# Row factors out of the gates' small rooms, branch weights behind gates, the last token tile's differences behind two up pairs

## The chip, the cores and the metric

The kernel runs on one core of a Trainium2 chip. The metric is device microseconds of one execution. A core has five engines with instruction queues of their own: TensorE (PE, matmuls; its weight loads are shown as PEld), VectorE (DVE), ScalarE (ACT), GpSimd (POOL) and SyncE (SP), which here only issues DMAs. An instruction waits at the head of its queue for semaphores, and everything behind it on that engine waits with it. Matmul results go to PSUM, which has eight banks of 128 x 512 fp32 here.

## The reference

One encoder layer on 1024 tokens of width 1024, fp32:

```
h = rmsnorm(x, g_mix)
z = h @ w_in                       # pool channels | q | k | v
y_pool = pool_mixer(z[:, :512])    # windows 2, 4, 8, 16: mean - self, per-group linear map, scale
y_attn = diff_attention(q, k, v)   # 8 heads, two softmax maps per head, difference, row-normalized
gates  = sigmoid(h @ w_gate + b_gate)
merged = gates[:, :1024] * (y_pool @ w_branch_pool) + gates[:, 1024:] * (y_attn @ w_branch_attn)
x = x + merged @ w_out
h2 = rmsnorm(x, g_ffn)
x = x + square(relu(h2 @ w_up)) @ w_down
```

## The kernel before

Everything is written in Python against a framework that makes the order of instructions of each engine itself: every instruction carries a priority (`tc.cur_priority`, which grows as the code is written and can be set), a scheduler picks by it and by its own model of when operands are there, and `tc.issue_after(e)` lets what is written inside its block stand only behind instruction `e` in that order. It is no wait for the end of `e`. Buffers are rooms of pools: a tile with a tag gets one of that tag's rooms, and waits until the readers of the room's last holder are done.

fp32 values are multiplied as three products of halves: `split` (L117 to L120) makes the high half by a cast on ACT (L119) and the low half by a subtraction on DVE or POOL (L120), and `mm3` (L125, L126, L127) issues three matmuls into one bank.

The stages, with their place in the profiled execution:

- norm, projections and attention head by head, up to about 700 us. The gates' pre-activations (names g, go) are made as filling work between heads, put into rooms that `tmp` hands out, and stored to DRAM (`g_dram`, L731 and L732). The row factors of a head, 1/norm of its output rows, are transposed (trr), copied (rT, L599) and stored to `r_dram` (L600).
- `y_scaled(d)` (L191 to L198) loads head d's output rows (ry) and its row factors broadcast to all partitions (rb) and multiplies them on DVE. `row_factors(d)` says where the factors lie: in one full room "fu" for d in 0, 1, 2, 3, 5, and in two halves of the small rooms (`tmp`: tags "fr" and "fo", two rooms of 512 columns each for this use) for 4, 6, 7.
- `branch_pool(d)` (L203 to L209), d = 0 to 7, is the pooling branch's product: bp, 192 matmuls from 703.5 to 746.75. Each half of 512 tokens is multiplied in PSUM by its gate on DVE: `mp = bp * gate` (L209). The gate half comes from `gate_half` (L825 to L830): a load from `g_dram` into a small room on SP (L826) and a sigmoid on ACT (L829). `load_cols2` (L145 to L154) brings branch weights for two d at a time (rbp, L148) and splits them on ACT and POOL.
- the attention branch's product, by seven products of sums and differences of quarters (Strassen's scheme): accumulators baX and baY from 747 us, operands wa (from wr, the branch weights) and yb (from ry). Its first accumulators use PSUM banks that bp products have held.
- the output projection (op, about 831 to 923), whose results are added to x in tiles y0 to y7 of 128 tokens, then the second norm. Tiles t = 0 to 3 go through `first_half`, 4 to 7 through `second_half` (L1161): the normalized tile is transposed on PE (hb, L1104) into two banks b12 and b22; `t1 = b12 - r11` and `t2 = b22 - t1` are the operands of two Strassen products; b12 and b22 are copied into the tile's own room (`kept_b`), and `b_split` writes high and low halves. `combine(q)` (L1177) later makes the operands T1, T3, 22 and T4 of tiles 4 to 7 from them; T4 loads d21 back (nd, L1191) into the tile's room.
- 16 up pairs (`up_pair`, a generator that stops twice on its way so that pairs can be interleaved): each is seven products X, Y, Z, W of a pair of column tiles of w_up (wu, L1228) with the quarters of h2, followed by relu, square and stores. X1 and Y (u11) use the quarters of tokens 0 to 511 only; the product with S2 uses T2, Z uses T1, the one with S3 uses T3, W uses 22 and the last T4.
- the down product (Da, Db) to the end.

In the code before, the loop over d writes the weight loads of d + 2 ahead of `branch_pool(d)`; and tiles 4 to 7 are taken one after another through `second_half` with the priorities of their output projections, after which the first steps of pairs 0 to 3 alternate with the four calls of `combine`.

Of the kernel before, what the change touches and what calls it, by code (L numbers as in the profile page):

```python
# [12 lines left out]
ALU = mybir.AluOpType  # L13
# [44 lines left out]
def encoder_kernel(  # L58
# [773 lines left out]
    def row_factors(d):  # L832
        return [fu_tile(f"rb{d}")] if d in (0, 1, 2, 3, 5) else [tmp(f"rb{d}_{i}") for i in range(2)]
# [109 lines left out]
    for d in range(NK):  # L943
        if d % 2 == 0 and d + 2 < NK:
            ws_bp[d + 2] = load_cols2(w_branch_pool, (d + 2) * P, f"bp{d + 2}", fw_tile)
        branch_pool(d, ws_bp[d - d % 2][d % 2], bank)
        if d == 1:
            for k in (6, 7):
                yr[k] = y_scaled(k, row_factors(k))
        if 1 < d < 6:  # L950
            with tc.issue_after(loaded[f"g{d - 1}_1"]):
                load_wr((2, 6, 3, 7)[d - 2])
        if d in (4, 6):
            first_weight_sums(d // 2)
        if d > 4:
            load_a(d - 5)
        if d > 2:
            split_b(d - 3)
# [202 lines left out]
    def second_half(t):  # L1161
        c0 = (t - 4) * P
        t1, t2 = (ev(f"{n}_{t}", (P, 4, P)) for n in ("t1", "t2"))
        T1s[t] = t1
        nc.sync.dma_start(t1, nd[0, t - 4])
        b12, b22 = norm_token(t, lambda j, name: bm.tile([P, 512], F32, tag="ZWY"[j], name=name))
        last["dve"] = dve.tensor_tensor(t1, b12, t1, op=ALU.subtract).ins
        sub(dve, t2, b22, t1)
        kept_b[t] = y[t].rearrange("p (q a b) -> p q a b", q=2, a=4)
        nc.scalar.copy(kept_b[t][:, 0], b12)  # L1170
        nc.scalar.copy(kept_b[t][:, 1], b22)
        b_split("T2", c0, t2, dve)
# [50 lines left out]
    def up_pair(p):  # L1223
# [12 lines left out]
        nc.scalar.copy(x1, X)  # L1236
# [3 lines left out]
        def finish(q, ps, part):  # L1240
            r = ev(f"u{q}_{p}")
            add(dve, r, ps, part)
# [56 lines left out]
    for t in range(4, NT):  # L1299
        tc.cur_priority = prio[min(t + 1, NT - 1)]  # L1300
        second_half(t)
    tc.cur_priority = now
    AHEAD = 4
    for p, q in zip(range(AHEAD), ("T1", "T3", "22", "T4")):
        next(pairs[p])
        if q == "T1":
            next(pairs[0])
        if q == "T3":
            body = tc.cur_priority
        with ExitStack() as behind:  # L1310
# [199 lines left out]
```

## Time and profile before

| | |
|---|---|
| median of 3 runs | 1547.08 us (1545.67 to 1551.84) |
| the profiled execution, its own time | 1546.83 us |
| span of its instructions | 1545.0 us |
| PE busy | 1517.9 us (98%), 7601 matmuls |
| DVE, ACT, POOL busy | 1065.1, 824.6 and 328.2 us |

The span is the time from the first to the last instruction in the profile, 1.83 us shorter than the execution. In the timelines a row is start and duration in us, engine, line, operation, output <- inputs, shape and count, and in brackets how long the engine had been idle and what released it; "SPq" and "ACTq" rows are DMA issues. In the list of waits a row has total, number and longest wait in us. Window rows have the stretch, its length, busy us with instruction counts of PE, PEld, DVE, ACT and POOL, the granted clock, the share of the DMA engines and GB/s. Rows of DMA issues end with KB each and the median us from issue to landing. Matmuls are pipelined: a duration of 0.39 us goes with a distance of 0.225 us from one to the next.

### The profile page before, as it was taken

What the parts mean: (1) busy time and instruction counts of PE and PEld (TensorE: products, weight loads), DVE (VectorE), ACT (ScalarE), POOL (GpSimd) and SP (SyncE); (2) the same over time, 40 slices, a digit from 0 to 9 for tenths busy, and PEclk for the clock granted to TensorE, in tenths of its full rate; (3) what the DMA queues carried; (4) which work ended last, traced back from release to release, by engine and by line L of the source; (5) the groups of instructions that cost most, each with busy time, mean ns of one, the idle gap of its engine ahead of it and who ended that gap; (6) DMA issues with size and microseconds to landing.
All of it is one profiled execution on the core that took longest, in us unless ns stands there. A gap on an engine that the chain in (4) does not pass through costs nothing.

```text
span 1545.0 us, 22233 instructions
## 1 busy us (share of the span) xinstructions
PE 1517.9 (98%) x7601; PEld 1312.5 (85%) x7601; DVE 1065.1 (69%) x2361; ACT 824.6 (53%) x1821; POOL 328.2 (21%) x476
## 2 busy tenths in 40 slices
PE   7999999999999999999899998999999999999998
PEld 6999999899999999788688887888888888888887
DVE  7777777778788887844678648766666668556672
ACT  6666565666565666543464556556555634333331
POOL 6654572434343334221000112000000000000000
PEclk9999999999999999999999999999999999999999
DMA  7331331111212022536455733555343699537750
GB/s 244 119 110 59 100 103 49 58 55 44 66 37 75 20 73 78 203 103 225 143 204 186 252 109 122 177 174 174 133 140 109 238 335 392 192 123 258 225 191 28
DMA packets 172045, 221.12 MB, mean 143 GB/s; under 512 B 10950, under 2 KB 104859, under 8 KB 171931
## 3 DMA queue, kind: packets, MB, share of 16 engines
q1 hardware_dynamic: 154522, 192.39, 37.8%
q10 hardware_dynamic: 17408, 27.30, 4.7%
q8 instruction: 60, 0.98, 0.3%
q14 instruction: 55, 0.44, 0.1%
HBM read 157.76 MB, written 61.90 MB: 142 GB/s over the span
## 4 chain that ended last, share of the span: by engine, by line
PE 90%; DMA 4%; DVE 3%; issue 1%; ACT 1%; SPq 0%; POOL 0%; ACTq 0%; DVEq 0%; POOLq 0%
PE z L127 6%; PE z L125 6%; PE z L126 6%; PE Da L125 4%; PE Da L126 4%; PE Da L127 4%; PE g L125 3%; PE g L126 3%; PE g L127 3%; PE Db L126 3%; PE Db L125 3%; PE Db L127 3%; PE X L125 3%; PE X L127 3%; PE X L126 3%; PE sc L486 2%
## 5 line engine op out<-in xcount | busy, mean ns | idle before, releaser
L127 PE MATMUL z<-wqkv,hT 128*128 128x384 f32 x512 | 174.3, 341 | 0.6 <-DVE hT L120 0.6
L125 PE MATMUL z<-wqkv,hT 128*128 128x384 f32 x512 | 174.6, 342 | 0.1
L126 PE MATMUL z<-wqkv,hT 128*128 128x384 f32 x512 | 174.3, 341 | 0.0
L496 ACT ACTIVATE s<-s,nm 128x256 f32<-128x256 f32 (+7 forms) x128 | 99.7, 779 | 69.9 <-DVE nm L488 61.5
L125 PE MATMUL g<-hT,fwgate 128*128 128x512 f32 x256 | 100.8, 394 | 0.7 <-ACT go L731 0.7
L126 PE MATMUL g<-hT,fwgate 128*128 128x512 f32 x256 | 100.6, 393 | 0.0
L125 PEld LDWEIGHTS z<-wqkv,hT 128*128 128x128 f32 x512 | 96.9, 189 | 3.8 <-ACT hT L119 0.4
L127 PE MATMUL g<-hT,fwgate 128*128 128x512 f32 x256 | 99.9, 392 | 0.0
L127 PEld LDWEIGHTS z<-wqkv,hT 128*128 128x128 f32 x512 | 96.8, 189 | 3.5 <-DVE hT L120 1.7
L126 PEld LDWEIGHTS z<-wqkv,hT 128*128 128x128 f32 x512 | 96.9, 189 | 3.2
L234 POOL TENSOR_TENSOR ms<-ms,mhalf 128x4 f32<-128x4 f32 x64 | 67.4, 1052 | 129.0 <-DVE ms L233 117.2
L488 DVE CUSTOM_DVE_ANT_0 s<-sc,dist 128x512 f32<-128x512 f32 (+3 forms) x128 | 74.8, 586 | 13.2 <-PE sc L486 11.3
L120 DVE TENSOR_TENSOR AS<-s,AS 128x512 fp32r<-128x512 f32 x64 | 43.8, 688 | 35.0 <-ACT AS L119 34.9
L485 PE MATMUL sc<-K,Q 128*128 128x512 f32 (+2 forms) x192 | 67.2, 359 | 0.3 <-DVE nm L488 0.3
L486 PE MATMUL sc<-K,Q 128*128 128x512 f32 (+2 forms) x192 | 65.2, 353 | 0.0
L120 POOL TENSOR_TENSOR wqkv<-rqkv,wqkv 128x384 fp32r<-128x384 f32 x60 | 61.5, 1038 | 13.3 <-ACT wqkv L119 10.1
L456 ACT CAST Q<-tk 64x128 fp32r<-64x128 f32 x128 | 33.1, 259 | 50.1 <-DVE K L455 48.7
L459 ACT CAST Q<-tk 64x128 fp32r<-64x128 f32 x128 | 33.3, 260 | 48.3 <-DVE Q L458 45.9
L125 PEld LDWEIGHTS g<-hT,fwgate 128*128 128x128 f32 x256 | 48.1, 188 | 9.3 <-ACT go L731 1.5
L433 POOL TENSOR_TENSOR qn<-qn,ggh 128x128 f32<-128x128 f32 x64 | 31.4, 490 | 115.4 <-DVE qn L427 83.1
L127 PEld LDWEIGHTS g<-hT,fwgate 128*128 128x128 f32 x256 | 48.1, 188 | 8.6
L126 PEld LDWEIGHTS g<-hT,fwgate 128*128 128x128 f32 x256 | 48.1, 188 | 8.3
(475 smaller groups left out, 4658.2 us busy)
## 6 DMA issues: line engine op xcount, KB each, us to landing
wd<-in_w_down_dram SPq DMA_DIRECT2D x56, 512.0 KB, 5.3
wu<-in_w_up_dram SPq DMA_DIRECT2D x32, 512.0 KB, 5.1
udS<-us SPq DMA_DIRECT2D x64, 256.0 KB, 2.1
ur<-udS SPq DMA_DIRECT2D x32, 512.0 KB, 4.4
rqkv<-in_w_in_dram SPq DMA_DIRECT2D x64, 192.0 KB, 2.9
ud<-u ACTq DMA_DIRECT2D x48, 256.0 KB, 4.3
ur<-ud SPq DMA_DIRECT2D x24, 512.0 KB, 5.3
frgate<-in_w_gate_dram SPq DMA_DIRECT2D x32, 256.0 KB, 3.2
```

Source lines behind the costliest of these rows:

```text
L120: return (lo_eng or nc.vector).tensor_tensor(lo, src, f(hi), op=ALU.subtract)
L125: nc.tensor.matmul(ps, lhs_hi, rhs_hi, start=first, stop=False, **kw)
L126: nc.tensor.matmul(ps, lhs_hi, rhs_lo, start=False, stop=False, **kw)
L127: nc.tensor.matmul(ps, lhs_lo, rhs_hi, start=False, stop=last, **kw)
L234: nc.gpsimd.tensor_tensor(dst, dst, mhalf[:, :n], op=ALU.pow)
L433: nc.gpsimd.tensor_tensor(qn[:, 2:4, :], qn[:, 2:4, :], ggh.unsqueeze(1).broadcast_to([P, 2, HD]), op=ALU.mult)
L456: nc.scalar.copy(q_hi, q)
L459: nc.scalar.copy(Q[other, m, 1, :], q)
L485: nc.tensor.matmul(dst, Q[:, i, 0, :], rhs, start=True, stop=False)
L486: nc.tensor.matmul(dst, Q[:, i, 1, :], rhs, start=False, stop=True)
L488: nc.vector.tensor_tensor_reduce(out=s[i][:, c : c + w], in0=sc[:, 0:w], in1=dist[:, o0 + c : o0 + c + w], scale=2.0 ** -(h + 1), scalar=B ...
L496: nc.scalar.activation(s[i][:, 0:n], s[i][:, 0:n], AF.Exp, bias=last, scale=-1.0, accum_out=Z[:, i, t : t + 1])
```

## The change

Three edits. (1) `row_factors(d)` gives every d one full tile, in turns from the rooms "fu" and "mx" (one each) of the pool fq; the small rooms hold gates only. (2) In the loop over d `branch_pool(d)` is written first, and the loads of the branch weights of d + 2 and d + 3 stand behind the load of gate half d_1. (3) `second_half(7)` gets the recording of pair 0 (two steps) and pair 1 (one step) between its norm and its differences; the differences, copies and splits of tile 7 stand behind pair 0's copy x1 and pair 1's sum u11, `combine("T1")` gets priorities ahead of pair 1, and T3, 22 and T4 stand behind the norm of tile 6 instead of that of tile 7.

```diff
@@ -830,7 +830,7 @@
         return gt
 
     def row_factors(d):
-        return [fu_tile(f"rb{d}")] if d in (0, 1, 2, 3, 5) else [tmp(f"rb{d}_{i}") for i in range(2)]
+        return [fq.tile([P, S], F32, tag=("fu", "mx")[d % 2], name=f"rb{d}")]
 
     ws_bp = {0: load_cols2(w_branch_pool, 0, "bp0", wt)}
     yr, mp, mT = {}, {}, {}
@@ -941,9 +941,10 @@
         t = hp1[i // 4].tile([P, 2, 512], F32, tag="H", name=f"mp{a_}_{th}")
         mp[a_, th], mp[a_ + 1, th] = t[:, 0, :], t[:, 1, :]
     for d in range(NK):
+        branch_pool(d, ws_bp[d - d % 2][d % 2], bank)
         if d % 2 == 0 and d + 2 < NK:
-            ws_bp[d + 2] = load_cols2(w_branch_pool, (d + 2) * P, f"bp{d + 2}", fw_tile)
-        branch_pool(d, ws_bp[d - d % 2][d % 2], bank)
+            with tc.issue_after(loaded[f"g{d}_1"]):
+                ws_bp[d + 2] = load_cols2(w_branch_pool, (d + 2) * P, f"bp{d + 2}", fw_tile)
         if d == 1:
             for k in (6, 7):
                 yr[k] = y_scaled(k, row_factors(k))
@@ -1158,18 +1159,22 @@
     kept_b = {}
     T1s = {}
 
-    def second_half(t):
+    def second_half(t, between=None):
         c0 = (t - 4) * P
         t1, t2 = (ev(f"{n}_{t}", (P, 4, P)) for n in ("t1", "t2"))
         T1s[t] = t1
         nc.sync.dma_start(t1, nd[0, t - 4])
         b12, b22 = norm_token(t, lambda j, name: bm.tile([P, 512], F32, tag="ZWY"[j], name=name))
-        last["dve"] = dve.tensor_tensor(t1, b12, t1, op=ALU.subtract).ins
-        sub(dve, t2, b22, t1)
-        kept_b[t] = y[t].rearrange("p (q a b) -> p q a b", q=2, a=4)
-        nc.scalar.copy(kept_b[t][:, 0], b12)
-        nc.scalar.copy(kept_b[t][:, 1], b22)
-        b_split("T2", c0, t2, dve)
+        behind = between() if between else ()
+        with ExitStack() as after_:
+            for e in behind:
+                after_.enter_context(tc.issue_after(e))
+            last["dve"] = dve.tensor_tensor(t1, b12, t1, op=ALU.subtract).ins
+            sub(dve, t2, b22, t1)
+            kept_b[t] = y[t].rearrange("p (q a b) -> p q a b", q=2, a=4)
+            nc.scalar.copy(kept_b[t][:, 0], b12)
+            nc.scalar.copy(kept_b[t][:, 1], b22)
+            b_split("T2", c0, t2, dve)
 
     kept_b["d21"] = ev("d21_7", (P, 4, P))
     nc.sync.dma_start(kept_b["d21"], nd[1, 3])
@@ -1233,13 +1238,13 @@
         Y = (bm if p % 2 else bx).tile([P, 512], F32, tag="Y", name=f"Y{p}")
         u_product(X, "1", a_op(p, "11", A["11"], dve))
         x1 = ev(f"x1_{p}")
-        nc.scalar.copy(x1, X)
+        last[f"x{p}"] = nc.scalar.copy(x1, X).ins
         u_product(Y, "2", a_op(p, "12", A["12"], dve))
         C = {}
 
         def finish(q, ps, part):
             r = ev(f"u{q}_{p}")
-            add(dve, r, ps, part)
+            last[f"u{q}_{p}"] = dve.tensor_tensor(r, ps, part, op=ALU.add).ins
             nc.scalar.activation(r, r, AF.Relu)
             nc.scalar.activation(r, r, AF.Square)
             C[q] = r
@@ -1296,21 +1301,35 @@
 
     pairs = [up_pair(p) for p in range(NP)]
     now = tc.cur_priority
-    for t in range(4, NT):
-        tc.cur_priority = prio[min(t + 1, NT - 1)]
+    for t in range(4, NT - 1):
+        tc.cur_priority = prio[t + 1]
         second_half(t)
-    tc.cur_priority = now
+    before_last = last["act"], last["dve"]
     AHEAD = 4
-    for p, q in zip(range(AHEAD), ("T1", "T3", "22", "T4")):
-        next(pairs[p])
-        if q == "T1":
-            next(pairs[0])
-        if q == "T3":
-            body = tc.cur_priority
+    body = [now, now]
+
+    def first_pairs():
+        here, tc.cur_priority = tc.cur_priority, now
+        next(pairs[0])
+        next(pairs[0])
+        body[0] = tc.cur_priority
+        tc.cur_priority += 40
+        next(pairs[1])
+        body[1] = tc.cur_priority
+        tc.cur_priority = here
+        return last["x1"], last["u11_1"]
+
+    second_half(NT - 1, first_pairs)
+    tc.cur_priority = body[0]
+    combine("T1")
+    assert tc.cur_priority < body[0] + 40
+    tc.cur_priority = body = body[1]
+    for p, q in zip(range(1, AHEAD), ("T3", "22", "T4")):
+        if p > 1:
+            next(pairs[p])
         with ExitStack() as behind:
-            if q != "T1":
-                for e in (last["act"], last["dve"]):
-                    behind.enter_context(tc.issue_after(e))
+            for e in before_last:
+                behind.enter_context(tc.issue_after(e))
             combine(q)
     norms.close()
     e2 = pool_of(hs, "e2", N_E2, side="right")
```

The change moves instructions at many places. SP's queue around the first gate loads, before (g1_0 is the first half of gate 1, rb row factors, rbp pooling branch weights, wr attention branch weights, rypT pooled rows):

```order
L826 DMA g1_0_8873<-g_dram_128 128x512
L826 DMA g1_1_8876<-g_dram_128 128x512
L872 DMA wr2_8965<-in_w_branch_attn_dram 128x1024
L187 DMA rypT2_8800<-p_dram_127 128x1024
L187 DMA rypT3_8808<-p_dram_127 128x1024
L148 DMA rbp2_8831<-in_w_branch_pool_dram 128x4x256
L148 DMA rbp4_8923<-in_w_branch_pool_dram 128x4x256
L148 DMA rbp6_9006<-in_w_branch_pool_dram 128x4x256
L826 DMA g0_0_8839<-g_dram_128 128x512
L826 DMA g0_1_8842<-g_dram_128 128x512
L197 DMA rb6_0_8907<-r_dram_126 128x512
L193 DMA ry6_8909<-y_dram_125 128x1024
```

and of the change:

```order
L826 DMA g0_1_8831<-g_dram_128 128x512
L187 DMA rypT2_8797<-p_dram_127 128x1024
L187 DMA rypT3_8805<-p_dram_127 128x1024
L148 DMA rbp2_8862<-in_w_branch_pool_dram 128x4x256
L197 DMA rb7_8909<-r_dram_126 128x1024
L826 DMA g1_0_8870<-g_dram_128 128x512
L826 DMA g2_0_8914<-g_dram_128 128x512
L826 DMA g1_1_8873<-g_dram_128 128x512
L872 DMA wr2_8956<-in_w_branch_attn_dram 128x1024
L193 DMA ry6_8905<-y_dram_125 128x1024
L826 DMA g2_1_8917<-g_dram_128 128x512
L148 DMA rbp4_8948<-in_w_branch_pool_dram 128x4x256
```

The loads of bp4 and bp6 leave their place ahead of gate 0 for one behind g2_1 and, further on, g4_1; gate 0 moves ahead of bp2's weights, wr2 behind gate 1, and rb7 ahead of gate 1. On ACT the copy of the last row factors and their store move behind the two casts of bp2's weights. DVE's rows in the small product part fall from eleven multiplications by row factors to eight.

DVE where pair 0 begins, before (t1_6 and t2_6 are tile 6's differences, A11_0 and A12_0 the low halves of pair 0's weights, y4 to y6 hold the kept banks of the tiles):

```order
L1167 TENSOR_TENSOR t1_6_10701<-hb6_0_10709,t1_6_10701 128x512
L120 TENSOR_TENSOR A11_0_10764<-wu0_0_10760,A11_0_10764 128x512
L120 TENSOR_TENSOR A12_0_10781<-wu0_0_10760,A12_0_10781 128x512
L1019 TENSOR_TENSOR t2_6_10702<-hb6_1_10710,t1_6_10701 128x512
L120 TENSOR_TENSOR A11_1_10815<-wu1_0_10811,A11_1_10815 128x512
L120 TENSOR_TENSOR A12_1_10832<-wu1_0_10811,A12_1_10832 128x512
L120 TENSOR_TENSOR A12_2_10885<-wu2_0_10864,A12_2_10885 128x512
```

and of the change:

```order
L1172 TENSOR_TENSOR t1_6_10692<-hb6_0_10700,t1_6_10692 128x512
L1020 TENSOR_TENSOR y4_10235<-y4_10235 128x512
L1020 TENSOR_TENSOR y5_10322<-y5_10322 128x512
L120 TENSOR_TENSOR A11_0_10749<-wu0_0_10745,A11_0_10749 128x512
L120 TENSOR_TENSOR A12_0_10766<-wu0_0_10745,A12_0_10766 128x512
L1020 TENSOR_TENSOR t2_6_10693<-hb6_1_10701,t1_6_10692 128x512
L120 TENSOR_TENSOR A11_1_10792<-wu1_0_10788,A11_1_10792 128x512
L120 TENSOR_TENSOR A12_1_10809<-wu1_0_10788,A12_1_10809 128x512
L120 TENSOR_TENSOR A12_2_10876<-wu2_0_10855,A12_2_10876 128x512
```

Two of T3's differences (y4 and y5, in place) now stand between t1_6 and the low half of A11_0.

DVE around tile 7's first difference t1_7, before:

```order
L120 TENSOR_TENSOR A11_2_10868<-wu2_0_10864,A11_2_10868 128x512
L120 TENSOR_TENSOR A11_3_10917<-wu3_0_10913,A11_3_10917 128x512
L1167 TENSOR_TENSOR t1_7_10730<-hb7_0_10739,t1_7_10730 128x512
L1019 TENSOR_TENSOR y4_10244<-y4_10244 128x512
L1019 TENSOR_TENSOR y5_10331<-y5_10331 128x512
L1019 TENSOR_TENSOR y6_10418<-y6_10418 128x512
L120 TENSOR_TENSOR B22l_10582<-y4_10244,B22h_10581 128x4x128
L120 TENSOR_TENSOR B22l_10582<-y5_10331,B22h_10581 128x4x128
L120 TENSOR_TENSOR B22l_10582<-y6_10418,B22h_10581 128x4x128
L1019 TENSOR_TENSOR t2_7_10731<-hb7_1_10740,t1_7_10730 128x512
L120 TENSOR_TENSOR BT1l_10578<-t1_7_10730,BT1h_10577 128x4x128
L120 TENSOR_TENSOR BT3l_10580<-y4_10244,BT3h_10579 128x4x128
```

and of the change:

```order
L1247 TENSOR_TENSOR u11_0_10781<-Y0_10748,x1_0_10764 128x512
L120 TENSOR_TENSOR A11_2_10859<-wu2_0_10855,A11_2_10859 128x512
L120 TENSOR_TENSOR B22l_10573<-y6_10409,B22h_10572 128x4x128
L120 TENSOR_TENSOR A11_3_10908<-wu3_0_10904,A11_3_10908 128x512
L120 TENSOR_TENSOR BT3l_10571<-y6_10409,BT3h_10570 128x4x128
L1247 TENSOR_TENSOR u11_1_10824<-Y1_10791,x1_1_10807 128x512
L120 TENSOR_TENSOR BT4l_10575<-y4_10235,BT4h_10574 128x4x128
L1172 TENSOR_TENSOR t1_7_10721<-hb7_0_10730,t1_7_10721 128x512
L120 TENSOR_TENSOR BT4l_10575<-y5_10322,BT4h_10574 128x4x128
L1020 TENSOR_TENSOR y6_10409<-y6_10409 128x512
L1020 TENSOR_TENSOR t2_7_10722<-hb7_1_10731,t1_7_10721 128x512
L120 TENSOR_TENSOR BT1l_10569<-t1_7_10721,BT1h_10568 128x4x128
```

Tile 7's t1 and its low split BT1l move behind u11_1, and T3's splits of tiles 4 to 6 ahead of it. On PE tile 7's transposes move 12 matmuls towards the front; between the second of them and pair 0's first Z matmul lie 44 matmuls (rows of X2, X3, Y2 and Y3) instead of 8. Pair 0's W, which came behind the first matmuls of its product with S3, now comes whole ahead of them.

More of the change, by code (lines that the diff above doesn't have):

```diff
@@ L1 @@
-from contextlib import ExitStack
+from contextlib import ExitStack, contextmanager
 import concourse.bass as bass
```

## The prediction, on record before the run

> **What bounds the kernel now.** I read the busy times first, then the waits of TensorE, then windows cut at these waits, then the timeline of each.
>
> ```profile
> span 1545.0 us, 22233 instructions
> PE 1517.9 (98%) x7601; PEld 1312.5 (85%) x7601; DVE 1065.1 (69%) x2361; ACT 824.6 (53%) x1821; POOL 328.2 (21%) x476
> ```
>
> TensorE is busy in 98% of the span; 1545.0 − 1517.9 = 27.1 us is idle. The edits remove no matmul, so what they bring has to come from this idle time or from matmuls slowed by it. Waits of TensorE (total, times, longest, us):
>
> ```profile
> PE hps L260 <- DVE hn L255: 8.4, 1, 8.4
> PE baX L125 <- DVE mp L209: 5.4, 4, 4.0
> PE X L125 <- ACT AS L119: 2.2, 1, 2.2
> PE Z L126 <- DVE BT1l L120: 2.1, 1, 2.1
> ```
>
> The first is the start, which the edits don't touch; the others lie where they do. The windows (stretch, length, busy us of PE, PEld, DVE, ACT, POOL, then clock, DMA share, GB/s) give the whole loss:
>
> ```profile
> 600.00:700.00 100.00, 98.15 (x509) 83.34 (x508) 65.52 (x178) 54.05 (x132) 26.06 (x30) 1.00 0.44 147
> 703.50:746.75 43.25, 43.25 (x192) 35.82 (x191) 28.53 (x40) 14.37 (x24) 8.18 (x6) 1.00 0.60 202
> 746.75:765.86 19.11, 13.71 (x50) 9.97 (x49) 9.42 (x15) 10.02 (x16) 0.00 (x0) 0.91 0.43 151
> 941.90:957.58 15.68, 11.34 (x50) 8.75 (x48) 15.68 (x28) 12.60 (x24) 0.00 (x0) 1.00 0.53 168
> ```
>
> The pooling product (703.5 to 746.75) runs without a gap: 43.25 / 192 = 0.225 us a matmul. The 50 matmuls behind it should take 11.26 us and take 19.11: **7.85 us lost**, 5.4 in waits and 2.45 in matmuls at a lower clock. The last 50 should take 11.27 and take 15.68: **4.4 us lost**, the two waits of 2.1 and 2.2.
>
> Stage one's timeline, ACT, DVE, PE and SP:
>
> ```profile
> 747.44 0.72 ACT L829 ACTIVATE g<-g,zero 128x512 f32<-128x512 f32 x1 [4.78 <-DVE mp L209]
> 752.58 0.72 ACT L829 ACTIVATE g<-g,zero 128x512 f32<-128x512 f32 x1 [1.58 <-DMA g<-g_dram]
> 755.18 1.28 DVE L209 TENSOR_TENSOR mp<-bp,g 128x512 f32<-128x512 f32 x2
> 755.92 0.80 PE L125 MATMUL baX<-yb,wa 128*128 128x512 f32 x1 [4.01 <-DVE mp L209]
> 757.79 0.63 PE L125 MATMUL baX<-yb,wa 128*128 128x512 f32 x1
> 759.04 0.40 PE L125 MATMUL baX<-yb,wa 128*128 128x512 f32 x1
> 739.09 8.70 SPq L826 DMA_DIRECT2D g<-g_dram  x5
> 748.91 7.93 SPq L826 DMA_DIRECT2D g<-g_dram  x4
> ```
>
> The attention product wants a PSUM bank that a gate product (mp) still reads; that product waits for a sigmoid, the sigmoid for a gate load, and SP issues the last gate loads at 739 to 757, long after the gates were stored, as their rooms come free late. After the 4.01 us stall matmuls take 0.63 us for a while, then 0.40.
>
> **The change, part by part.** *Rooms and queue.* The factors of groups 4, 6 and 7 leave the small rooms, so a gate load waits for gate products alone: three loads fewer on SP, three DVE products fewer. What now stands ahead of each gate load on SP I walked with these prices:
>
> ```profile
> 700.09 0.29 ACTq L600 DMA_DIRECT2D r_dram<-rT  x1
> 702.01 0.62 ACT L119 CAST wbp<-rbp 128x512 fp32r<-128x512 f32 x1 [1.95 <-DMA rbp<-in_w_branch_pool_dram]
> 707.99 0.33 ACTq L732 DMA_DIRECT2D g_dram<-go  x1
> g<-g_dram SPq DMA_DIRECT2D x18, 256.0 KB, 3.8
> ry<-y_dram SPq DMA_DIRECT2D x2, 512.0 KB, 5.7
> rbp<-in_w_branch_pool_dram SPq DMA_DIRECT2D x3, 512.0 KB, 3.4
> g_dram<-go ACTq DMA_DIRECT2D x4, 256.0 KB, 2.9
> ```
>
> The last factors' store now stands behind the casts of bp2's weights, so at about 703.4 instead of 700.1; landed 2.9 later at most (the last row, a store of that queue), it lets rb7 go by 706.3. Behind rb7 stand g1, g2 and wr2. g1_1 needs the room from which the last pre-activation is stored (707.99, landed 2.9 later at 710.9, later still if that store is slow): I have it go at 712.3, and wr2 at 712.8. wr2's 512 KB land 5.7 later, and DVE splits wr2 ahead of the product mp1_0, which comes at 719.5. From there the gates are taken two rooms at a time, and by my walk mp4_0 ends near 738 and mp6_1 near 744; mp7_1 is held by TensorE alone and ends at 747.5. The third and fourth attention products need their banks at 748.5 and 749.4: no wait, with some 1 to 2 us to spare. Gain 7.85; I take **7.2**, leaving 0.65 for a short wait. Bounds: 7.85, and the cover's end below.
>
> *Weights behind gates.* rbp4 now follows g2_1 on SP, rbp6 follows g4_1. Each still has to land (3.4), be cast (0.62) and split on POOL:
>
> ```profile
> 725.07 1.28 POOL L120 TENSOR_TENSOR wbp<-rbp,wbp 128x512 fp32r<-128x512 f32 x1 [14.14 <-ACT wbp L119]
> 735.76 1.52 POOL L120 TENSOR_TENSOR wbp<-rbp,wbp 128x512 fp32r<-128x512 f32 x1 [9.41 <-ACT wbp L119]
> ```
>
> By the walk bp4's first half is split at 722.6 and wanted at 725.4, bp6's at 734.0 and wanted at 736.3. So 2.8 and 2.3 us cover it: cost 0, and each us beyond is a us of TensorE. This is the weakest cover of the sum.
>
> *Token 7's differences.* Before, DVE had token 7's t1 ahead of its low splits, and Z waited for it; now it stands behind pair 1's u11, and 44 matmuls lie between its transposes and the first Z where 8 lay (at 0.225, 9.9 us against 1.8):
>
> ```profile
> 938.24 0.60 PE L1104 MATMUL hb<-identf,y 128*128 128x128 f32 x4
> 938.88 0.69 DVE L1167 TENSOR_TENSOR t<-hb,t 128x512 f32<-128x512 f32 x1 [4.36 <-PE hb L1104]
> 943.69 0.68 DVE L120 TENSOR_TENSOR BT1l<-t,BT1h 128x512 fp32r<-128x512 f32 x1
> 944.43 0.50 PE L126 MATMUL Z<-BT1l,AS 128*128 128x512 f32 x1 [2.15 <-DVE BT1l L120]
> 957.58 0.50 PE L125 MATMUL X<-BT3h,AS 128*128 128x512 f32 x1 [2.20 <-ACT AS L119]
> ```
>
> BT1l needs about 944.4 again, Z now comes at 948.5: 4 us of cover. The second wait goes since W now stands whole ahead of X's T3 product, as the order of matmuls shows; A22's split, by the walk, ends 1.5 us before W needs it. Gain **4.4**. A cost: two T3 differences now stand ahead of the first low split on DVE, which has no slack:
>
> ```profile
> 925.10 1.28 DVE L120 TENSOR_TENSOR A<-wu,A 128x512 fp32r<-128x512 f32 x2
> 925.84 0.19 PEld L127 LDWEIGHTS X<-B11h,A 128*128 128x128 f32 x1 [0.15 <-DVE A L120]
> 941.29 1.89 DVE L120 TENSOR_TENSOR B22l<-y,B22h 128x512 fp32r<-128x512 f32 x3
> ```
>
> At some 0.6 us each (1.89 / 3) the split ends at 927.0 instead of 925.8, and TensorE stands **1.2 us** at the third matmul of pair 0. Bounds 0 (DVE idles ahead of t1_6 and might take them early) and 1.9.
>
> The Trainium skill ("TensorE: Matmul & The Clock Gate", Part 1: The HAM clock gate) says that an idle window of about 3.4 us halves the clock for as long. The trace agrees: 0.63 us behind the 4.01 us stall, 0.50 then 0.40 behind those of 2.1 and 2.2. By that rule the new stall of 1.2 us costs only itself, and any stall left in stage one that stays under 3.4 would lose no clock; the sum stays as it is.
>
> *Elsewhere.* Before 700 the scheduler's order moves too; the window of 600 to 700 holds 1.85 us of idle TensorE. I take 0, bounds −1.85 and +1.85.
>
> Sum: −7.2 − 4.4 + 1.2 = **−10.4**. The profiled execution took 1546.83 (span 1545.0, 1.83 around it), so 1536.4; the median, 1547.08, lies 0.25 higher: **1536.5**.
>
> **The rivals.**
>
> *A. Weights late.* If a gate chain is a few us later than walked (POOL's splits spread from 1.28 to 1.52 here), bp6 waits: 5 us late costs 2.7, 8 us costs 5.7. For it: rbp4 and rbp6 went out at 698 to 706 before, and now wait for products. Against: 2.3 us of cover. Time 1539 to 1543, say 1541.
>
> *B. The gain is given back at the output weights.*
>
> ```profile
> ACT wo L119 <- DMA ro<-in_w_out_dram: 12.1, 4, 5.1
> ```
>
> ACT waits up to 5.1 us for w_out. If those loads keep their clock time, of the 7.85 won some 3.5 come back as a wait near 830: 1540. Against: they are issued behind the gates on the same queue, so they should come earlier too, and no PE wait is there now.
>
> *C. SP stands still (slower).* rb7 now stands ahead of g1, g2, wr2 and rbp4 and waits for a store behind the casts of bp2's weights, which wait for a load on SP itself. A delay d there delays every gate and both weight loads; TensorE pays d − 2.3 and can't be covered, since its next work is the same product. All of 10.4 is gone at d = 12.7, and at d = 16 the time is 1550. Against: one landing here takes 2.9 to 5.7, so d of 16 needs three in a row.
>
> *D. The gates stay late* because something else (wr's split, sigmoids) sets their pace: stage two alone stays, −4.4 + 1.2 = −3.2, so 1543.9. For it: ACT waited 4.78 for DVE's mp, not only for loads.
>
> **How the numbers follow.** Forecast (1534.5 to 1538.5) 0.60; A 0.19; B 0.10; D 0.05; C 0.06. What lies within 0.5% (7.7 us) can't be told from no change; faster means below 1539.3. Faster: 0.60 and a fifth of A: 0.64. Slower: C, 0.06. Same: the rest, 0.30. The range 1533.5 to 1544: below, the forecast less 1.85 and the 1.2 stall not coming; above, A, B and D. It leaves out C and some edges, under 2 in 10.
>
> **What would show it.** Right: no wait of baX for mp, and clock 1.00 in the 50 matmuls behind the pooling product; mp1_0 near 719.5; no wait of Z for BT1l; a new wait of about 1.2 us for A's low split at the third matmul of pair 0. Wrong: TensorE waiting for wbp's split inside the pooling product (A or C), wo's wait growing and reaching op (B), or baX still behind mp (D). A wait anywhere else on TensorE of more than 2 us would mean that I missed a mover.

## The result

The changed kernel takes 1535.57 us (median of 6 runs, 1535.19 to 1536.37) against 1547.75 us of the kernel before (6 runs). The ratio is 0.9919, with a 95% interval of 0.9906 to 0.9932: 0.8% faster. 1536.5 had been predicted. Two executions of later comparisons, 2550.75 us of the kernel before and 3937.29 us of the kernel with edits 1 and 2, stand apart from all others and are in none of the ratios.

The head of the page of the changed kernel, and its waits of TensorE (total, times, longest in us):

```profile
span 1534.0 us, 22224 instructions
PE 1514.5 (99%) x7601; PEld 1311.1 (85%) x7601; DVE 1063.2 (69%) x2358; ACT 825.3 (54%) x1821; POOL 329.4 (21%) x476
```

```profile
PE hps L260 <- DVE hn L255: 10.2, 2, 9.1
...
PE X L127 <- DVE A L120: 0.9, 1, 0.9
...
PE Y L125 <- DVE u L1247: 0.8, 1, 0.8
```

The wait of 5.4 us of baX for mp, the 2.1 us of Z for BT1l and the 2.2 us of X for AS are gone. Two smaller ones have come at pair 0 and pair 2: 0.9 us for A's low split, which the prediction had, and 0.8 us of Y for u, which it had not. (The first row is the start of the kernel, which the edits don't touch.)

Windows of the changed kernel over the pooling product, the 50 matmuls behind it and token 7's place (columns as before):

```profile
703.83:747.12 43.29, 43.29 (x192) 35.85 (x191) 29.58 (x43) 15.64 (x25) 6.17 (x4) 1.00 0.71 253
747.12:758.23 11.11, 11.11 (x51) 9.20 (x49) 5.87 (x9) 6.63 (x11) 0.00 (x0) 1.00 0.15 48
916.00:935.00 19.00, 17.26 (x83) 13.88 (x82) 18.73 (x29) 12.24 (x24) 7.54 (x5) 1.00 0.21 59
935.00:955.00 20.00, 20.00 (x90) 16.57 (x89) 20.00 (x34) 15.29 (x29) 0.00 (x0) 1.00 0.62 194
```

What took 19.11 us at a clock of 0.91 takes 11.11 at 1.00 without a gap. At token 7's place 1.74 us of TensorE are idle instead of 4.3; both waits that are left end with an instruction of DVE, and DVE is busy without a gap from 935 to 955.

Where the time went can be read from the first and last start of a product. Before and after (line, engine, operation, count: ns min/median/max, first and last start in us):

```profile
L125 PE MATMUL bp<-ypT,wbp x64: 389/389/389, 703.5 to 746.3; 128*128 128x512 f32 x64
L125 PE MATMUL baY<-yb,wa x48: 389/389/389, 765.9 to 819.6; 128*128 128x512 f32 x48
L125 PE MATMUL X<-B11h,A x64: 387/389/481, 924.5 to 1204.6; 128*128 128x512 f32 x64
L125 PE MATMUL Da<-w_0h,u_0h x32: 389/389/499, 1235.2 to 1501.9; 128*128 128x512 f32 x32
```

```profile
L125 PE MATMUL bp<-ypT,wbp x64: 389/389/389, 703.8 to 746.7; 128*128 128x512 f32 x64
L125 PE MATMUL baY<-yb,wa x48: 389/389/389, 758.2 to 811.9; 128*128 128x512 f32 x48
L125 PE MATMUL X<-B11h,A x64: 389/389/481, 916.9 to 1194.2; 128*128 128x512 f32 x64
L125 PE MATMUL Da<-w_0h,u_0h x32: 389/389/504, 1224.8 to 1491.4; 128*128 128x512 f32 x32
```

From the first bp to the first baY (stage one below) 62.4 us have become 54.4: **8.0 us**. From the first X to the first Da (stage two) 310.7 have become 307.9: **2.8 us**. The first bp starts 0.3 later, and between the last Da and the end of the span 0.5 is gained; together 11.0, the difference of the spans (1545.0 and 1534.0). These two lengths, which hold within 0.1 us from profile to profile of the changed kernel (54.4, 54.4, 54.4 and 307.9, 308.0, 308.0 in three), tell edits apart better than the times do. A fall of the clock is in them, though: where TensorE's granted clock dropped in the profiled execution, the stage holds that loss too (stage one of before and of weights_only and weights_last, stage two of weights_only and t3_behind_u).

Both stages in us as the profiles of all runs give them, with the median time of each (in brackets the name under which the expectations speak of it):

| kernel | stage one | stage two | median, us |
|---|---|---|---|
| before | 62.4 | 310.7 | 1547.75, 1550.72, 1547.91, 1548.80 and 1550.28 beside the runs |
| changed (later change_again, change_third) | 54.4 | 307.9 | 1535.57, later 1535.51 and 1536.31 |
| edit 1 alone (rooms_only) | 54.4 | 310.8 | 1538.50 |
| edit 2 alone (weights_only) | 62.5 | 312.2 | 1549.74 |
| edits 1 and 2 (gates_both) | 54.4 | 311.1 | 1537.55 |
| edit 3 alone (token_only) | 59.2 | 308.0 | 1545.47 |
| weights later (weights_later) | 55.9 | 308.0 | 1538.14 |
| weights last (weights_last) | 63.6 | 308.0 | 1544.57 |
| T3 behind u11_0 (t3_behind_u) | 54.4 | 309.7 | 1534.37 |
| T3 behind u11_1 (t3_behind_u1) | 54.4 | 307.7 | 1536.34 |
| T3 behind u11_0, T4's low splits on POOL (pool4_u) | 54.4 | 307.6 | 1534.90 |
| the same, A22 early (early22_p) | 54.4 | 307.0 | 1534.78 |

### The profile page after: what moved, and what is told of

It reads as the page before. It is cut to its first block, busy times and chain, and to the rows that moved or that the text cites. A ratio compares the mean times of both kernels' runs of the same rounds, so it can differ in the third digit from the quotient of the medians.

```text
span 1534.0 us, 22224 instructions
## 1 busy us (share of the span) xinstructions
PE 1514.5 (99%) x7601; PEld 1311.1 (85%) x7601; DVE 1063.2 (69%) x2358; ACT 825.3 (54%) x1821; POOL 329.4 (21%) x476
## 4 chain that ended last, share of the span: by engine, by line
PE 92%; DVE 3%; DMA 3%; SPq 1%; issue 1%; ACT 1%; POOL 0%; DVEq 0%; ACTq 0%
PE z L125 5%; PE z L127 5%; PE z L126 5%; PE Da L125 4%; PE Da L126 4%; PE Da L127 4%; PE g L125 3%; PE g L127 3%; PE g L126 3%; PE Db L126 3%; PE Db L125 3%; PE Db L127 3%; PE X L127 3%; PE X L126 3%; PE X L125 3%; PE sc L485 2%
## 5 line engine op out<-in xcount | busy, mean ns | idle before, releaser
L125 PE MATMUL z<-wqkv,hT 128*128 128x384 f32 x512 | 174.5, 341 | 0.1
L126 PE MATMUL z<-wqkv,hT 128*128 128x384 f32 x512 | 174.0, 340 | 0.0
L127 PE MATMUL z<-wqkv,hT 128*128 128x384 f32 x512 | 173.8, 340 | 0.0
L125 PE MATMUL g<-hT,fwgate 128*128 128x512 f32 x256 | 100.8, 394 | 0.9 <-ACT go L731 0.9
L126 PE MATMUL g<-hT,fwgate 128*128 128x512 f32 x256 | 100.6, 393 | 0.0
L127 PE MATMUL g<-hT,fwgate 128*128 128x512 f32 x256 | 100.3, 393 | 0.0
L125 PEld LDWEIGHTS z<-wqkv,hT 128*128 128x128 f32 x512 | 96.6, 189 | 3.6 <-DVE qn L427 0.3
L126 PEld LDWEIGHTS z<-wqkv,hT 128*128 128x128 f32 x512 | 96.7, 189 | 3.2
L127 PEld LDWEIGHTS z<-wqkv,hT 128*128 128x128 f32 x512 | 96.6, 189 | 2.4 <-DVE hT L120 0.5
L120 POOL TENSOR_TENSOR wqkv<-rqkv,wqkv 128x384 fp32r<-128x384 f32 x60 | 62.6, 1057 | 13.1 <-ACT wqkv L119 9.7
L125 PEld LDWEIGHTS g<-hT,fwgate 128*128 128x128 f32 x256 | 48.1, 188 | 9.3 <-ACT go L731 1.5
L127 PEld LDWEIGHTS g<-hT,fwgate 128*128 128x128 f32 x256 | 48.1, 188 | 8.8
L126 PEld LDWEIGHTS g<-hT,fwgate 128*128 128x128 f32 x256 | 48.1, 188 | 8.2
```

Source lines behind the costliest of these rows:

```text
L120: return (lo_eng or nc.vector).tensor_tensor(lo, src, f(hi), op=ALU.subtract)
L125: nc.tensor.matmul(ps, lhs_hi, rhs_hi, start=first, stop=False, **kw)
L126: nc.tensor.matmul(ps, lhs_hi, rhs_lo, start=False, stop=False, **kw)
L127: nc.tensor.matmul(ps, lhs_lo, rhs_hi, start=False, stop=last, **kw)
```

## The experiments

**Which edit carries stage one: the rooms.** Edit 1 alone, in the kernel before:

```diff
-        return [fu_tile(f"rb{d}")] if d in (0, 1, 2, 3, 5) else [tmp(f"rb{d}_{i}") for i in range(2)]
+        return [fq.tile([P, S], F32, tag=("fu", "mx")[d % 2], name=f"rb{d}")]
```

> The kernel before with the row factors alone moved into one full tile each; the branch weights keep their place ahead of the gates, token 7 keeps its order. Theory R (the small rooms hold the last gates up): the whole loss of stage one goes, TensorE waits for no mp, and the time is 7.2 to 8.0 us below the kernel before, about 1539.5; the waits of 2.1 (Z for BT1l) and 2.2 us (X for AS) stay. Rival Q (the place of the weight loads on SP's queue is what holds the gates up): the third of these loads stands on SP ahead of gate 1 until its room is free, at 705.7 before, so the last gates stay late and at most 3 us are won, 1544 to 1547.

1538.50 us, ratio 0.9935 (0.9917 to 0.9954); the kernel before had 1550.72 beside it, so the times alone give more than the 7.2 to 8.0 that were written. Its waits of TensorE between 930 and 965 (there is none between 700 and 760):

```profile
PE Z L126 <- DVE BT1l L120: 2.1, 1, 2.1
PE W L125 <- ACT A L119: 1.6, 1, 1.6
```

What the last gate loads waited for stands in SP's own waits between 695 and 760. Two of their rows before:

```profile
SPq L826 <- DVE mp L209: 21.1, 10, 6.2
SPq L826 <- DVE ry L198: 7.9, 4, 4.8
```

The second row is gate loads that stand until a multiplication by row factors (ry, L198) has let go of a room: 7.9 us in four waits. With edit 1 alone that row is gone, and the gate loads wait for gate products (mp). Stage one has its full 8.0 us with the weights' loads in their old place, so rival Q falls. (Edit 1 also makes three loads and three DVE products fewer; what part of the 8.0 is theirs was not tried apart.) SP does stand at the third of these loads, as Q had it, but only until 704.5, and goes on with gate 1:

```profile
696.64 3.64 SPq L148 DMA_DIRECT2D rbp<-in_w_branch_pool_dram  x2
704.03 0.34 SPq L197 DMA_DIRECT2D rb<-r_dram  x1
704.47 0.39 SPq L148 DMA_DIRECT2D rbp<-in_w_branch_pool_dram  x1
704.90 6.49 SPq L826 DMA_DIRECT2D g<-g_dram  x3
```

That is 3 us later than in the changed kernel (its three gate loads start at 701.98), and it does not matter. Of the two waits at token 7 one stays; in the other's place W waits 1.6 us for A.

Edit 2 alone, in the kernel before:

```diff
+        branch_pool(d, ws_bp[d - d % 2][d % 2], bank)
         if d % 2 == 0 and d + 2 < NK:
-            ws_bp[d + 2] = load_cols2(w_branch_pool, (d + 2) * P, f"bp{d + 2}", fw_tile)
-        branch_pool(d, ws_bp[d - d % 2][d % 2], bank)
+            with tc.issue_after(loaded[f"g{d}_1"]):
+                ws_bp[d + 2] = load_cols2(w_branch_pool, (d + 2) * P, f"bp{d + 2}", fw_tile)
```

> The kernel before with the branch weights' loads alone behind the gates; factors of groups 4, 6 and 7 stay in the small rooms. R: no gain, 1546 to 1549, as gate loads still wait for rooms that row factors hold, and the wait of baX for mp stays within 1.5 us of 5.4. Q: 4 to 8 us are won, 1539 to 1543.

1549.74 us, ratio 0.9999 (0.9987 to 1.001): no gain, as R had it. But R's reason was wrong in part: the wait of baX for mp did not stay at 5.4, it is gone. Its waits between 700 and 760, and the window over the pooling product:

```profile
PE bp L127 <- POOL wbp L120: 3.5, 2, 2.9
PE bp L125 <- ACT wbp L119: 1.4, 3, 0.7
```

```profile
707.05:758.00 50.95, 45.96 (x191) 36.35 (x190) 29.80 (x44) 18.03 (x28) 10.77 (x6) 0.97 0.68 232
```

With gates that still wait for rooms, weights behind them come late: bp2's load leaves at 712.83 instead of 698.54, behind a gate load for which SP stood 13.1 us until a store of pre-activations had landed, and SP waits for products with row factors as before (8.7 us in four waits). The wait moves into the pooling product: 50.95 us for what takes 43.25. The time is also 0.7 us above what R wrote. This is rival A of the prediction, and the changed kernel escapes it only since edit 1 has let the gates go. Stage two, which this edit doesn't touch, is 1.5 us longer by a fall of the clock behind the wait of Z; the last section shows it. The two edits together without the third:

> Edits 1 and 2 without the one at token 7. By the prediction edit 2 is worth nothing: the same as rooms_only (1538.5) within 0.8 us, and 2.5 to 3.3 us above the changed kernel. Rival: the weights behind the gates let gate 1 go earlier and win 1 us or more against rooms_only.

1537.55 us, ratio 0.9924 (0.9909 to 0.9939); stage one is 54.4 with edit 2 and without. By the median it is 0.95 us below edit 1 alone and 2.0 above the changed kernel beside it, both outside what was written (0.8, and 2.5 to 3.3); it was not run beside edit 1 alone. The stage lengths show no gain against edit 1 alone, and stage two, 3.1 longer than in the changed kernel beside it (311.1 and 308.0), lies inside the second range. Edit 2 is worth nothing that these profiles show.

**Edit 3 alone**, in the kernel before (the hunks of the diff from `second_half` on):

> Only the third edit (token 7's differences behind the first steps of pairs 0 and 1). If the two stages are separate, the waits of 2.1 and 2.2 us go, those of about 0.9 (X for A's low split) and 0.8 us (Y for u11) that the changed kernel shows come, and the time is 2.5 to 3.3 us below the kernel before, about 1544.5; the wait of baX for mp stays at about 5.4. If the gain at token 7 needs the earlier gates (less work left on DVE or ACT behind them), less than 1.5 us is won.

1545.47 us, ratio 0.9967 (0.9953 to 0.9981), 5.2 us below the kernel before beside it, more than was written; stage two is 308.0, 2.7 below before, with the same two waits of 0.9 and 0.8. The stages add: 8.0 + 2.7 = 10.7, where the changed kernel has won 10.8 in both. What was not expected is stage one, 59.2 instead of 62.4 in a kernel whose stage one is untouched. Its wait behind the pooling product:

```profile
PE baX L125 <- DVE mp L209: 3.7, 4, 2.8
```

and two matmul rows of its timeline, where the longest part of it ends:

```profile
754.56 0.50 PE L125 MATMUL baX<-yb,wa 128*128 128x512 f32 x1 [2.82 <-DVE mp L209]
755.13 0.62 PE L127 MATMUL baX<-yb,wa 128*128 128x512 f32 x2
```

The stall was 2.8 us in this execution, not 4.0, and the clock did not fall behind it. This execution was the fastest of the ten, 1540.92 us at a mean clock of 1.000; the nine others had 0.997 or 0.998. (The 0.62 in the last row is of two matmuls.) The loss of stage one in the kernel before is thus not one number; the section on the hardware comes back to it.

**How long the weights could wait.** Two kernels moved the last weights' load back, to price the cover that the prediction called the weakest. First bp4's behind g3_1 and bp6's behind g5_1:

```diff
-        if d % 2 == 0 and d + 2 < NK:
+        if d in (0, 3, 5):
             with tc.issue_after(loaded[f"g{d}_1"]):
-                ws_bp[d + 2] = load_cols2(w_branch_pool, (d + 2) * P, f"bp{d + 2}", fw_tile)
+                n = (d + 2) // 2 * 2
+                ws_bp[n] = load_cols2(w_branch_pool, n * P, f"bp{n}", fw_tile)
```

> The changed kernel with the loads of bp4's weights behind gate half g3_1 instead of g2_1, and bp6's behind g5_1 instead of g4_1: by the changed kernel's trace 6.2 and 7.1 us later. By the cover that this trace shows (first half of bp4 split at 719, wanted at 725.6; of bp6 at 731.2, wanted at 736.4) bp4 is hidden and bp6 costs 1 to 3 us: 1536.5 to 1538.5. By the cover of the prediction's walk (2.8 and 2.3 us) the two cost 4.8 us together, 1540.4. If weights' loads are no part of the path at all, 1535.5.

1538.14 us, one new wait:

```profile
PE bp L125 <- ACT wbp L119: 1.2, 1, 1.2
```

bp6's load went out at 732.89 instead of 723.48, 9.4 us later, and cost 1.2: about 8.2 us of cover (9.4 − 1.2), where the prediction's walk had 2.3 and the reading of the changed kernel's trace in the expectation 5.2. Both counted until POOL's low half is there; the wait ends with ACT's high half. The order of matmuls has moved with it: behind the wait only L125 and L126 stand at first, which use the weights' high half, where in the changed kernel L125, L126 and L127 alternate from the start. So 8.2 is the cover of the kernel with the later load; the changed kernel's own is 5.7 (low half split at 731.2, first L127 at 736.92). Then bp6's load behind g6_1, with gate 6 loaded ahead of it:

```diff
-        gs_ = [gate_half(d, th) for th in range(2)]
+        gs_ = early.pop(d, None) or [gate_half(d, th) for th in range(2)]
...
+        if d == 5:
+            early[6] = [gate_half(6, th) for th in range(2)]
-        if d % 2 == 0 and d + 2 < NK:
-            with tc.issue_after(loaded[f"g{d}_1"]):
+        if d in (0, 2, 5):
+            with tc.issue_after(loaded["g6_1" if d == 5 else f"g{d}_1"]):
...
```

> The changed kernel with the load of bp6's weights behind gate half g6_1 (gate 6 is loaded ahead of it). In weights_later this load went out at 732.9 and TensorE waited 1.2 us; behind g6_1, which goes out at 737.6 to 739 there, it is 5 to 6.5 us later, so TensorE waits 6 to 8 us for wbp inside the pooling product and the time is 5 to 8 us above the changed kernel from the wait alone, 1541 to 1543.5. If a long stall also lets the clock fall, 1.5 to 2.5 us come on top in those runs where it does, with a mean clock of 0.999 or less and matmuls of about 0.63 us behind the stall. If late weights are made up behind (gates' work hides there), less than 4 us is lost.

1544.57 us, beside 1536.31 of the changed kernel in the same comparison: 8.3 us more. TensorE's wait and the rows behind it, and the window that holds them:

```profile
743.99 0.80 PE L125 MATMUL bp<-ypT,wbp 128*128 128x512 f32 x1 [6.04 <-ACT wbp L119]
744.58 0.63 PE L126 MATMUL bp<-ypT,wbp 128*128 128x512 f32 x1
745.01 0.63 PE L125 MATMUL bp<-ypT,wbp 128*128 128x512 f32 x1
...
749.70 0.49 PE L127 MATMUL baX<-yb,wa 128*128 128x512 f32 x1
```

```profile
745.00:770.00 25.00, 25.00 (x101) 20.45 (x100) 8.59 (x14) 9.36 (x16) 1.52 (x2) 0.90 0.21 75
```

Each us past the cover is a us of TensorE, as rival A had it. Counted from the first bp of each kernel, this load went out 14.1 us later than the changed kernel's; less 8.2 of cover that makes 5.9, and the wait is 6.0. The lower clock comes on top: the 13 matmuls from 743.99 to 749.70 take 5.7 us instead of 2.9, so 2.8 us. The two make 8.8 of the 9.2 us by which stage one is longer in this profile; the medians differ by 8.3. All ten runs had a mean clock of 0.996 to 0.999.

**What is left at token 7.** The two new waits were to go if T3's differences stood behind pair 0's u11_0 on DVE:

```diff
-            for e in before_last:
+            for e in before_last + (last["u11_0"],):
                 behind.enter_context(tc.issue_after(e))
```

> The changed kernel with the operands T3, 22 and T4 behind pair 0's sum u11_0 as well as behind token 6's norm, so that no difference of T3 stands ahead of the first low split or of u11_0 on DVE. If these differences are what TensorE's new waits of 0.9 and 0.8 us come from, both go and the time is 1.0 to 1.7 us below the changed kernel, 1534.2. If DVE is simply full there, the waits move to a later operand (BT3l, A22) and the time stays within 0.5 us or rises.

> The changed kernel itself, beside the kernel before on this chip, where the latter ran from 1544.91 to 1553.62 in the runs above with mean granted clocks of 1.000 to 0.995. If that spread comes from the stall behind the pooling product (long enough in some runs to let the clock fall, 2.8 us and no fall in the profile of token_only), the changed kernel has it not: clock 1.000, all runs within 2 us, 1535 to 1536.5, and the gain here is 12 to 16 us. If the spread is the chip's, the changed kernel spreads by 5 us or more too.

The changed kernel in the same comparison took 1535.51 us (1535.25 to 1537.31), with a mean clock of 1.000 in all five runs and 12.4 us below the kernel before beside it; this one took 1534.37 (1533.55 to 1536.81). The two waits are gone, and another is there, with a clock that falls behind it:

```profile
945.69 0.50 PE L125 MATMUL W<-BT4h,A 128*128 128x512 f32 x1 [1.42 <-ACT A L119]
946.69 0.50 PE L125 MATMUL X<-BT3h,AS 128*128 128x512 f32 x1 [0.27 <-ACT U L1268]
...
947.49 0.63 PE L125 MATMUL X<-BT3h,AS 128*128 128x512 f32 x1
...
950.48 0.58 PE L126 MATMUL X<-BT3l,AS 128*128 128x512 f32 x1
950.89 0.39 PE L127 MATMUL X<-BT3h,AS 128*128 128x512 f32 x1
```

1.4 + 0.3 stands where 0.9 + 0.8 stood: the waiting has only moved to A22, an operand that the rival named. Stage two, 309.7 in this profile, includes the lower clock, some 1.7 us; without it, it would be about 308.0, no shorter than the changed kernel's. The median is 1.1 us lower, as the theory had it, and the runs of the two overlap. The profiled execution was the slowest of the five and the only one with a mean clock under 1.000, so what gave the other four their time isn't shown. With the operands behind u11_1:

> As t3_behind_u, but behind pair 1's u11_1. The same two waits go; T3's and T4's operands come 2 to 4 us later than there, with at most 1.5 us of cover before W and X by the walk of the prediction. Theory: 1.0 to 1.7 us below the changed kernel as well if cover holds; rival: a wait of 1 to 2 us of X for BT3l or W for A22, no gain.

1536.34 us, no gain. X waits 1.7 us for AS, the operand made of S3's halves and not one that was named: again the same sum at another place.

A full DVE was the suspect, so the four low splits of T4 went to POOL, on top of the edit that put T3 behind u11_0:

```diff
-                b_split(q, c0, d21, dve)
+                b_split(q, c0, d21, pool)
```

> t3_behind_u with the four low splits of T4 on POOL, which stands idle there, instead of DVE: DVE gets 4 x 0.6 = 2.4 us of room between tile 6's differences and pair 0's W. If a full DVE is what keeps moving the wait (0.9 and 0.8 us in the changed kernel, 1.4 and 0.3 in t3_behind_u), TensorE waits less than 0.5 us between 915 and 955 and the time is 1.2 to 2.0 us below the changed kernel, about 1533.7. If POOL's slower splits (1.3 to 1.5 us each for this shape elsewhere) come too late for W, a wait for BT4l of 0.5 to 2 us takes their place and nothing is won.

> The changed kernel beside the two others, to compare with: 1535 to 1536.5, clock 1.000 in all runs or nearly all, waits of about 0.9 and 0.8 us at token 7's place.

1534.90 us (1533.83 to 1536.56) beside 1536.31 of the changed kernel (1535.64 to 1537.04). No wait for BT4l came, but W still waited, 1.2 us, for A22's cast on ACT. The median is 1.4 us lower, inside the range, but stage two only 0.4, so the time doesn't bear the theory out. DVE did not get its 2.4 us of room either. While POOL splits, DVE's rows are longer (the kernel with DVE's splits has 0.68 or 0.69 for the same rows):

```profile
936.61 4.72 POOL L120 TENSOR_TENSOR BT4l<-y,BT4h 128x512 fp32r<-128x512 f32 x3 [7.61 <-ACT BT4h L119]
937.00 1.46 DVE L1020 TENSOR_TENSOR y<-y 128x512 f32<-128x512 f32 x1
938.38 0.68 DVE L1020 TENSOR_TENSOR t<-hb,t 128x512 f32<-128x512 f32 x1
938.98 1.18 DVE L120 TENSOR_TENSOR BT1l<-t,BT1h 128x512 fp32r<-128x512 f32 x1
```

Two more are 1.19 (at 940.69) and 1.78 (at 944.20, beside POOL's fourth split). The four together are some 2.9 us longer than at 0.68, about what the move was to free. ACT's rows tell why W waited:

```profile
944.38 0.63 ACT L1249 ACTIVATE u<-u 128x512 f32<-128x512 f32 x1
946.75 0.62 ACT L119 CAST AS<-s 128x512 fp32r<-128x512 f32 x1 [1.73 <-DVE s L1020]
947.27 0.61 ACT L119 CAST A<-wu 128x512 fp32r<-128x512 f32 x1
```

A22's cast needs nothing but weights that are there; it stood behind S3's cast, for which ACT waited 1.73 us. So A22's split was recorded ahead of S3, its low half on POOL, on top of the two edits before:

```diff
+        a22 = a_op(p, "22", A["22"], pool) if p == 0 else None
         sub(dve, S3, A["11"], A["21"])
...
-        u_product(W, "4", a_op(p, "22", A["22"], dve))
+        u_product(W, "4", a22 or a_op(p, "22", A["22"], dve))
```

> pool4_u with the split of pair 0's A22 recorded ahead of S3 and its low half on POOL. In pool4_u the cast of A22 stood on ACT behind the cast of S3, for which ACT waited 1.73 us, and TensorE's W waited 1.2 us for it. If that queue order is the whole of the last wait, no wait over 0.4 us is left between 915 and 955, stage two lasts some 1.2 us less than in pool4_u (277.0 us from the first to the last X of the first product there), and the time is 1533 to 1534.5. If DVE sets the pace whatever stands where, X waits about 1 us for S3's halves instead and the time stays at 1534.9.

No wait is left between 915 and 955 us; one of 0.5 us (Z for u, at 958) is. The time came out 0.3 us above the range that was written for it, and the stage lost 0.6 us where 1.2 was written (276.4 us from the first to the last X of the first product, 277.0 in pool4_u; stage two 307.0 and 307.6). Stage two is 0.9 to 1.0 below the changed kernel. The time, 1534.78 us (1533.83 to 1535.41), ratio to before 0.9902 (0.9886 to 0.9917), is lower than the changed kernel's medians by 0.7 to 1.5 us. It was not timed beside the changed kernel, and its interval overlaps that kernel's (0.9897 to 0.9928 and 0.9902 to 0.9932 in the later comparisons): that it beats it is shown by stage two in the trace, by the times only made likely. That W's wait came from the queue order of ACT holds; that DVE sets the pace whatever stands where does not, though DVE is without a gap from 930 to 945 in this kernel too.

## Why the prediction was right, and where it was off

*Stage one, −7.2, measured −8.0.* The mechanism was as described: rooms held by row factors set the last gates, the gate products the banks, and TensorE waited for them. Edit 1 alone gives all 8.0. The 0.65 held back for a short wait was not needed. The walk to the gate products was right in its order and too late in its times: mp1_0 was put at 719.5 and starts at 713.85, the last factors' store at 703.4 and goes at 700.33, wr2's load at 712.8 and goes at 708.36. It started from the old time of bp2's weights; SP issued them at 695.55 rather than 698.54 (696.64 with edit 1 alone; what made them earlier was not tried apart), and all behind came earlier. The 2.9 us that it gave the store "at most" is a median of four in the row it was read from. Of the loss itself it put 2.45 us down to a lower clock; the window's 0.91 over 19.11 us makes 1.7 of it, and the other 0.7 is not clock by that figure; likely it is how rows around a wait are recorded (0.50 us and more for the matmul right behind one). The 7.85 stand all the same. At the end the walk was good: mp7_1 ends at 748.2 (747.5 predicted), bank wanted at about 749.4.

*Weights behind gates, 0, measured 0*, with a cover mis-sized: 2.3 us stood there; the changed kernel has 5.2 by the same reckoning, and with the load moved back TensorE stood only after about 8.2. The error was on the careful side and is why rival A got 0.19; its price per us was right (6.0 of wait for 5.9 past the cover), but a stall of that length also cost 2.8 us of clock, which A's sum left out.

*Stage two, −4.4 + 1.2, measured −2.8.* The two old waits went as written, the new stall at the third matmul of pair 0 came, at 0.9 instead of 1.2. What the sum missed is a second price of the same edit: besides these two differences, seven more operations of T3, 22 and T4 (three differences and four splits) now stand ahead of u11_0 on DVE, and pair 2's Y, which wants u11_0's bank, waited 0.8 us:

```profile
931.12 0.68 DVE L1247 TENSOR_TENSOR u<-Y,x 128x512 f32<-128x512 f32 x1
931.85 0.50 PE L125 MATMUL Y<-B21h,A 128*128 128x512 f32 x1 [0.81 <-DVE u L1247]
```

With T3, 22 and T4 behind u11_0 both waits were gone. The prediction looked at the operand next in line, not at what else DVE owed TensorE behind it.

*Rivals.* B (the output weights take the gain back) did not come: stage one's 8.0 us are there in full at the first op. C (SP stands at rb7) did not: rb7 went out at 701.56, and the gate loads right behind it. D fell with edit 1 alone, where no wait for mp is left.

*The rest.* The terms make −10.4, the spans differ by 11.0: stage one gave 0.8 more than its term, stage two 0.4 less, the end behind the last Da another 0.5, and the first bp came 0.3 later. The medians differ by 12.2, as the median of before was 1547.75 in the comparison and not 1547.08, and the changed kernel's lies lower against its profiled execution; the last section has the likely cause. That the time came within 0.9 us of the forecast is in part luck: the errors of the terms go both ways.

*The page's rule* ("TensorE: Matmul & The Clock Gate", Part 1: The HAM clock gate, in the Trainium skill) was read in the prediction as: no stall under 3.4 us loses clock. The runs contradict that reading: the clock fell for 3.4 us (947.49 to 950.9) behind waits of 1.4 and 0.3 us, and behind single waits of 2.14 and 2.44 us in the kernel with edit 2 alone. In the changed kernel the stall of 0.9 did cost only itself, so the sum was not hurt; with waits of 2.1 us that went either way, this was not sure beforehand.

## What to carry to other kernels

A load that issues late is first asked which room it waits for, and who else uses that room; moving loads around in the queue without that won nothing here and moved the wait into the pooling product. Where an engine without a gap owes TensorE several operands, the wait that is removed comes back at the next operand; what took the last one away here was to look for an instruction that needs nothing and stands behind one that waits. Moving splits from DVE to POOL gave DVE no room that the trace shows. And the length of a stage between two of its matmuls, read from profiles, settles tenths of a us which medians that spread by 2 us cannot.

## What the runs showed of the hardware

The kernel before spreads by 8.7 us (1544.91 to 1553.62 in the comparisons), the changed kernel by 2.1 (1535.19 to 1537.31 over 16 runs). The mean granted clock of each run goes with it: of 44 runs of the kernel before, 15 had a mean clock of 0.995 and a mean time of 1551.9 us, 11 had 0.996 and 1549.8, 11 had 0.997 and 1547.5, four had 0.998 and 1548.4, two had 0.999 and 1546.5, and the one with 1.000 took 1544.91. All 16 runs of the changed kernel had 0.999 or 1.000. So the gain is some 9.4 us where both have the full clock (1544.91, a single run, and 1535.5) and some 16 where the kernel before has 0.995. The kernel with edit 1 alone, which lacks the stall of stage one, ran at 0.999 and 1.000 in its four runs; the one with edit 3 alone, which keeps it, at 0.997 to 1.000. In which stalls the runs at 0.995 lost their clock isn't shown, as the one profiled execution of the kernel before had 0.999 and a single fall.

How long a stall has to be for that isn't settled by its length alone. The clock held behind 2.8 us (edit 3 alone, above), and fell behind 4.0 us (the kernel before), 6.0 us, 2.4 us and 1.4 + 0.3 us. The plainest case is one and the same wait, Z for BT1l: it took 2.15 us in the kernel before and 2.14 with edit 1 alone, and the matmuls behind it were at 0.40 us or less soon after. In the kernel with edit 2 alone it took 2.14 too, and the clock fell:

```profile
947.98 0.79 PE L126 MATMUL Z<-BT1l,AS 128*128 128x512 f32 x1 [2.14 <-DVE BT1l L120]
948.57 0.63 PE L127 MATMUL Z<-BT1h,AS 128*128 128x512 f32 x1
```

In the same way W's and X's 1.6 + 0.3 us with edit 1 alone cost no clock, where 1.4 + 0.3 did above. The case of 2.4 us is in the kernel with edit 2 alone too, in the attention part ahead of 700 us:

```profile
644.03 0.47 PE L541 MATMUL ta<-identf,s 128*128 128x128 f32 x1 [2.44 <-DVE AT_0l L120]
...
644.80 0.63 PE L485 MATMUL sc<-K,Q 128*128 128x512 f32 x1
...
647.63 0.40 PE L127 MATMUL g<-hT,fwgate 128*128 128x512 f32 x1
```

A fall costs 1.5 to 2.8 us here: a clock of 0.91 over the 19.11 us of the kernel before (1.7 us), 1.5 us of stage two with edit 2 alone, 2.8 with the longest stall, and 0.83 over 10 us (1.7 us) where T3 stands behind u11_0:

```profile
945.00:955.00 10.00, 9.05 (x31) 7.02 (x32) 10.00 (x18) 6.56 (x13) 0.00 (x0) 0.83 0.63 182
```

The Trainium skill's page on TensorE and the clock gate, in the section named above, says that the window in which activity is watched runs free, which would let the same stall fall on it in one run and not in another; the waits of Z above agree with that, and no run here tests it.

DVE beside POOL is the other point. In the kernel with T4's low splits on POOL the four stretched rows of DVE (1.18 to 1.78 us instead of 0.68) overlap a split of POOL and read nothing from a PSUM bank; the rows at 938.38 and 940.09, which overlap one too but read the banks hb and Y, kept 0.68. The kernel with A22 early shows the same at the same rows (1.45, 0.68 and 1.18). Two profiles show this; no run was made to test it.
